# Separate tiles for the samples' keys and values in a two-layer hybrid decoder step

## The chip, the core and the metric

The kernel is written in Bass with the Tile framework and runs on one NeuronCore of one Trainium2 chip. The metric is the device time of one launch in microseconds. One execution was also recorded by the hardware profiler; all rows below come from that recording.

## What is computed

The reference is one inference step of a two-layer trunk for two groups of tokens that share the weights: a prompt of 256 tokens and 8 samples of one token each with a past of 1024 tokens. In each layer:

```python
x += g1 * W_out [ NSA(h) ++ SSD(h) ],  h = RMSNorm(x) * (1 + s1) + b1
x += g2 * ConvFFN(RMSNorm(x) * (1 + s2) + b2)
```

The scales and shifts come from a modulation projection of a conditioning vector (the `ada` weights). NSA is attention with 8 query heads over 2 key/value heads of width 64 in three branches: compressed blocks, selected blocks and a sliding window, mixed by gates. For a sample, the selected branch reads 1024 past positions (8 pages of 128 positions, addressed through a page table, in an order that differs for each sample) with one block of 64 masked off by the selection, and the sliding branch reads a stored state of 512 positions. SSD is a Mamba-2 scan with 8 heads, 2 groups of B and C and a state of 64; for a sample it is one step: the state of 8 x 64 x 64 is decayed, the outer product of x and B is added, and the result is read with C. The outputs are the two groups of tokens and all new states; the sliding state is among them, so every sample's stored keys and values are copied to an output as well as read.

## The kernel before

All arithmetic is at float32 accuracy. The large projections split each operand into a rounded high part and a remainder (`split`, one ScalarE and one VectorE instruction, type float32r) and do three matmuls for each product of 128 x 128 weights with 264 tokens. Smaller products, among them everything in the samples' attention, are plain float32 matmuls, which the profiler shows as two records each.

A layer (`layer`) runs: the norm; a projection for gates; 6 tiles of the convolved x/B/C (a loop over `m`); 10 tiles of keys, values and queries (a second loop over `m`); the attention and state-space stretch; the half of the output projection that depends on the attention; the second norm; and the feed-forward stage with its 44 up-projection and 22 down-projection tiles. In both loops over `m`, `next(side, None)` issues the next pair of modulation weights (two loads of 512 KB and 16 small matmuls), and `next(first, None)` does the next unit of the samples' compressed keys and values (`compress`). In layer 0 these units run inside the loops, on a pool `cmp0` of their own which `done()` closes behind the second loop; then the pool `attn0` opens in its place. In layer 1 the units have run in the feed-forward stage of layer 0, and `attn1` opens at the start of the layer. The modulation weights use two or three buffers, depending on the pool.

The attention and state-space stretch is written as Python generators: `samples` (S), `prompt` (P), `blocks` (B), `gating` (Z), the state space with its gate and output projection (M), and modulation (A). A string of letters, `SEQ`, tells which generator advances next. This is the program order. The framework's scheduler then orders each engine's instructions ahead of the run: among those that its cost model holds ready, the one that is earliest in program order goes first, so that a load can be issued well ahead of its place in the source. On the chip each engine, and each queue that issues transfers (SP for loads, GpSimd for stores), runs that fixed order and waits at an instruction whose inputs or buffer are not there. All scheduling helpers record their instructions from one line, L117, so the rows below are told apart by tile names: `psat`, `psmm`, `pso` and `psfl` are the accumulation banks, `page` the samples' keys and values, `qz` their queries, `mam` the masked B and C, `ada` and `cpg` modulation weights and compressed pages, `st` the weight tiles, `wst` the sliding state, `slcc` the paged cache.

The samples' attention goes through three stages `i`: pages 0 to 3, pages 4 to 7, and the sliding state. Each stage needs a tile of keys and values for each of the 8 samples (`fetch`, 512 KB): four page loads of 128 KB each, every one behind a register load of its page number, or one load of 512 KB from the sliding state, which is at once stored to the output from the same tile. There are 8 such tiles. `scores(i)` does 8 matmuls of a sample's queries (32 columns) with 512 positions, into four groups of 32 output partitions; `values(i)` does 64 small matmuls and, after each half of the samples, fetches the tiles of the next stage into the buffers just read.

## Time and profile before

| | |
|---|---|
| median of 3 runs | 1052.64 us (1051.48 to 1057.06) |
| profiled execution | 1040.78 us, of which the recorded span is 1039.0 us |
| mean granted TensorE clock | 0.945 of full speed |
| TensorE / VectorE / ScalarE / GpSimd busy | 949.7 / 650.7 / 487.4 / 167.8 us |
| HBM read / written | 204.70 / 14.25 MB |

Busy shares are averages over stages with different limits. Granted clock 1.00 is 2.4 GHz, 0.50 is 1.2 GHz. PE is TensorE, PEld its weight loads, DVE VectorE, ACT ScalarE, POOL GpSimd; SPq and POOLq are the queues on which SP and GpSimd issue transfers.

### The profile page before, as it was taken

What the parts mean: (1) busy time and instruction counts of PE and PEld (TensorE: products, weight loads), DVE (VectorE), ACT (ScalarE), POOL (GpSimd) and SP (SyncE); (2) the same over time, 40 slices, a digit from 0 to 9 for tenths busy, and PEclk for the clock granted to TensorE, in tenths of its full rate; (3) what the DMA queues carried; (4) which work ended last, traced back from release to release, by engine and by line L of the source; (5) the groups of instructions that cost most, each with busy time, mean ns of one, the idle gap of its engine ahead of it and who ended that gap; (6) DMA issues with size and microseconds to landing.
All of it is one profiled execution on the core that took longest, in us unless ns stands there. A gap on an engine that the chain in (4) does not pass through costs nothing.

```text
span 1039.0 us, 21345 instructions
## 1 busy us (share of the span) xinstructions
PE 949.7 (91%) x7864; PEld 803.7 (77%) x7864; DVE 650.7 (63%) x1429; ACT 487.4 (47%) x1042; POOL 167.8 (16%) x337
## 2 busy tenths in 40 slices
PE   4599998988997998999999989998999799999996
PEld 2368997653585998999999868875447599999995
DVE  1386643867677665676754575485665687777553
ACT  1356543533444555555634344454244366666441
POOL 2000100225221101001101112031421221111110
PEclk9699999999997999999999989997599899999998
DMA  9987488246757786756675578725283835666651
GB/s 357 313 278 266 158 265 292 94 129 225 270 171 254 232 301 216 238 194 220 210 251 174 183 279 301 244 83 158 91 354 96 330 124 182 183 183 183 194 163 42
DMA packets 101258, 220.35 MB, mean 212 GB/s; under 512 B 11682, under 2 KB 54562, under 8 KB 101026
## 3 DMA queue, kind: packets, MB, share of 16 engines
q1 hardware_dynamic: 97058, 205.28, 59.8%
q0 software_dynamic: 3520, 13.17, 3.1%
q8 instruction: 62, 1.02, 0.4%
q10 hardware_dynamic: 576, 0.54, 0.2%
q14 instruction: 42, 0.34, 0.1%
HBM read 204.70 MB, written 14.25 MB: 211 GB/s over the span
## 4 chain that ended last, share of the span: by engine, by line
PE 76%; DMA 11%; DVE 7%; ACT 3%; issue 2%; SPq 1%; POOL 0%; DVEq 0%; ACTq 0%; POOLq 0%
PE psmm L117 40%; PE psat L117 22%; PE pso L117 10%; PE psfl L117 4%; DMA st<-in_cw_dram 3%; DMA ada<-in_ada_dram 3%; DVE wlo L117 2%; DMA cpg<-in_ada_dram 2%; DMA st<-in_wup_dram 1%; DMA page<-in_wst_dram 1%; DVE s L117 1%; SPq L117 1%; ACT whi L117 1%; DVE rs L117 1%; ACT psc L117 1%
## 5 line engine op out<-in xcount | busy, mean ns | idle before, releaser
L117 DVE TENSOR_TENSOR wlo<-st,whi 128x1024 fp32r<-128x1024 f32 (+1 forms) x204 | 232.7, 1142 | 152.6 <-ACT whi L117 149.1
L117 ACT ACTIVATE whi<-st 128x1024 fp32r<-128x1024 f32 (+1 forms) x204 | 201.6, 990 | 217.5 <-PE psmm L117 150.2
L117 PE MATMUL psmm<-hhi,whi 128*128 128x264 f32 x800 | 233.7, 293 | 3.3 <-ACT whi L117 1.4
L117 PE MATMUL psmm<-hhi,wlo 128*128 128x264 f32 x800 | 228.5, 286 | 1.1 <-DVE wlo L117 1.1
L117 PE MATMUL psmm<-hlo,whi 128*128 128x264 f32 x800 | 228.2, 286 | 0.0
L117 PEld LDWEIGHTS psmm<-hhi,whi 128*128 128x128 f32 x800 | 151.4, 189 | 17.0 <-ACT whi L117 5.2
L117 PEld LDWEIGHTS psmm<-hhi,wlo 128*128 128x128 f32 x800 | 150.9, 189 | 5.2 <-DVE wlo L117 2.4
L117 PEld LDWEIGHTS psmm<-hlo,whi 128*128 128x128 f32 x800 | 151.5, 190 | 2.4 <-issue 2.0
L117 PE MATMUL psmm<-act,whi 128*128 128x264 f32 x704 | 128.5, 284 | 0.0
L117 PEld LDWEIGHTS psmm<-act,whi 128*128 128x128 f32 x704 | 108.9, 188 | 1.6 <-issue 1.6
L117 PE MATMUL psat<-hhi,whi 128*128 128x264 f32 x352 | 100.8, 286 | 2.2 <-ACT whi L117 2.2
L117 PE MATMUL psat<-hhi,wlo 128*128 128x264 f32 x352 | 100.5, 286 | 1.0 <-DVE wlo L117 1.0
L117 PE MATMUL psat<-hlo,whi 128*128 128x264 f32 x352 | 100.6, 286 | 0.0
L117 PE MATMUL psmm<-act,wlo 128*128 128x264 f32 x352 | 99.9, 284 | 0.0
L117 PE MATMUL pso<-whi,cwh 128*128 128x252 f32 x256 | 74.8, 292 | 8.7 <-ACT whi L117 8.0
L117 PE MATMUL pso<-wlo,cwh 128*128 128x252 f32 x256 | 74.1, 290 | 1.8 <-DVE wlo L117 1.8
L117 PE MATMUL pso<-whi,cwl 128*128 128x252 f32 x256 | 73.6, 287 | 0.0
L117 PEld LDWEIGHTS psat<-hhi,whi 128*128 128x128 f32 x352 | 67.1, 191 | 2.5 <-ACT whi L117 2.5
L117 POOL COPY fout<-xr 128x26 f32<-128x26 f32 x44 | 28.1, 639 | 247.0 <-ACT xr L117 247.0
L117 PEld LDWEIGHTS psat<-hhi,wlo 128*128 128x128 f32 x352 | 66.7, 190 | 1.2 <-DVE wlo L117 1.2
L117 PEld LDWEIGHTS psat<-hlo,whi 128*128 128x128 f32 x352 | 67.2, 191 | 0.0
L117 PEld LDWEIGHTS psmm<-act,wlo 128*128 128x128 f32 x352 | 66.1, 188 | 0.0
(305 smaller groups left out, 1579.5 us busy)
## 6 DMA issues: line engine op xcount, KB each, us to landing
st<-in_wup_dram SPq DMA_DIRECT2D x88, 512.0 KB, 3.9
ada<-in_ada_dram SPq DMA_DIRECT2D x80, 512.0 KB, 5.2
st<-in_wdn_dram SPq DMA_DIRECT2D x44, 512.0 KB, 3.6
st<-in_win_dram SPq DMA_DIRECT2D x40, 512.0 KB, 4.9
page<-in_slcc_dram SPq DMA_DIRECT2D x128, 128.0 KB, 2.7
cpg<-in_ada_dram SPq DMA_DIRECT2D x16, 512.0 KB, 9.4
st<-in_cw_dram SPq DMA_DIRECT2D x16, 512.0 KB, 5.9
cpg<-in_cmpc_dram SPq DMA_DIRECT2D x64, 128.0 KB, 3.7
```

The costliest lines, as they stand in the source:

```text
L117: ins = f(*a, **k)
```

## The change

Keys and values get tiles of their own: 8 of 256 KB for keys (`pk`) and 8 for values (`pv`), the same memory in all. `fetch(b)` loads one of them: four page loads of 64 KB, or half of the sliding state. The keys of the next stage are fetched as soon as a stage's scores have been computed, the values after `values` as before. The first 16 fetches (`prefetch`) are spread over both loops over `m`, and in layer 0 the compressed units are finished and `attn0` is opened at the second step of the second loop. The 8 score matmuls of a stage are issued as one unbroken run (`together`: the first is ordered as before, the others directly behind it, in reverse sample order, so that the run begins when the last tile is there). The stores of the sliding state are no longer issued with the load but after `values(2)`, in program order, 16 of 256 KB. The B and C rows of the samples are split into a high part and a remainder, 16 rows in place of 8, and broadcast by a one-pass float32r matmul in place of a float32 one. `SEQ` is as it was.

```diff
--- before.py
+++ after.py
@@ -92,6 +92,7 @@
     ov_n, ov_j = np.arange(NCMP), np.arange(16)
     add("overlap", (16 * ov_n[:, None] < 64 * ov_j[None] + 64) & (16 * ov_n[:, None] + 32 > 64 * ov_j[None]))
     add("sum4", np.tile(np.eye(32), (4, 1)))
+    add("eye8", np.tile(np.eye(8), (2, 1)))
     add("iota", np.broadcast_to(np.arange(16.0), (128, 16)))
     return np.concatenate(parts, 1)
 
@@ -498,23 +499,25 @@
 
 
         order = (0, 2, 4, 6, 1, 3, 5, 7)
-        ring = []
-
-        def fetch():
-            n = len(ring)
+        ring, kept = ([], []), []
+
+        def fetch(b):
+            n = len(ring[b])
             i, s = n // NS, order[n % NS]
             if i > 2:
                 return
-            t = ph([1024], "page", PAGES)
+            t = ph([512], ("pk", "pv")[b], NS)
             if i == 2:
-                load(t, I["wst"][l, s])
-                store(O["wst"][l, s], t)
-                v = t.rearrange("p (a c f) -> p a c f", a=2, c=4)
-                ring.append((v[:, 0], v[:, 1]))
+                load(t, I["wst"][l, s, :, 512 * b:512 * b + 512])
+                kept.append((O["wst"][l, s, :, 512 * b:512 * b + 512], t))
             else:
-                v = t.rearrange("p (c a f) -> p c a f", a=2, c=4)
-                load_pages(v, I["slcc"][l], s, 0, 2, 4 * i, 4)
-                ring.append((v[:, :, 0, :], v[:, :, 1, :]))
+                load_pages(t.rearrange("p (c a f) -> p c a f", a=1, c=4), I["slcc"][l], s, b, 1, 4 * i, 4)
+            ring[b].append(t.rearrange("p (c f) -> p c f", c=4))
+
+        def prefetch():
+
+            if len(ring[1]) < NS:
+                fetch(len(ring[0]) // NS)
 
 
         first = iter(()) if early is None else early()
@@ -568,6 +571,8 @@
                 next(side, None)
             for _ in range(EARLY):
                 next(first, None)
+            if pb is not None:
+                prefetch()
             o = mtile(I["win"][l, 10 + m], h)
             r = sb([291], "xr", 2)
             G.memset(r[:, 0:3], 0.0)
@@ -607,8 +612,12 @@
                 next(side, None)
             for _ in range(EARLY):
                 next(first, None)
-            if pb is not None and len(ring) < PAGES:
-                fetch()
+            if m == 5 and pb is None:
+                run(first)
+                done()
+                pb = begin("attn0")
+            if pb is not None:
+                prefetch()
             o = mtile(I["win"][l, m], h)
             if m < 4:
                 S.activation(q[:, m, :], o[:, :T], AF.Copy, scale=0.125)
@@ -626,11 +635,7 @@
             PE.transpose(o[:8, 256:384], kv[:, m, TP:], ident)
             S.activation(vt[:, b], o[:, :256].rearrange("p (t f) -> p t f", t=2), AF.Copy)
             S.activation(vn[:8, b], o[:8, 256:384], AF.Copy)
-        run(first)
         run(side)
-        if pb is None:
-            done()
-            pb = begin(f"attn{l}")
 
         def samples():
 
@@ -657,8 +662,8 @@
                           stop=s % 2 == 1)
             slf = small([2], 1, "slf")
             V.tensor_copy(slf, selfp[:, :2])
-            while len(ring) < PAGES:
-                fetch()
+            while len(ring[1]) < NS:
+                prefetch()
             pc = small([NCMP], 1, "pc")
             V.tensor_tensor(pc, sp_[:, :NCMP], K["cbias"], op=OP.add)
             st4 = small([8], 1, "st4")
@@ -708,9 +713,10 @@
 
             def scores(i, sc):
                 o = sx()
-                for n, s in enumerate(order):
-                    c = s // 2
-                    PE.matmul(o[32 * c:32 * c + 32, :], qz[:, s, :], ring[NS * i + n][0], start=s % 2 == 0, stop=s % 2 == 1)
+                together([(o[32 * (s // 2):32 * (s // 2) + 32, :], qz[:, s, :], ring[0][NS * i + n], s % 2 == 1, s % 2 == 0)
+                          for n, s in reversed(list(enumerate(order)))])
+                for _ in range(NS):
+                    fetch(0)
                 V.tensor_tensor(sc, sc, o, op=OP.add)
 
             def transposed(sc, pT):
@@ -731,10 +737,10 @@
                     for ch in range(4):
                         for c in range(4):
                             rows = slice(32 * c, 32 * c + 32)
-                            PE.matmul(Ov[rows, sp, :], pT[:, ch, rows], ring[NS * i + 4 * sp + c][1][:, ch, :],
+                            PE.matmul(Ov[rows, sp, :], pT[:, ch, rows], ring[1][NS * i + 4 * sp + c][:, ch, :],
                                       start=sp == 0 and ch == 0 and not cmp, stop=sp == 1 and ch == 3, skip_group_check=True)
                     for c in range(4):
-                        fetch()
+                        fetch(1)
                 if out is None:
                     out = small([128], 1, "ov" + "s-w"[i])
                     V.tensor_scalar(out, Ov[:, 0, :], K["rmask"][:, 0:1], None, op0=OP.mult)
@@ -802,6 +808,8 @@
             for _ in range(WAITS[4]):
                 yield
             ov = values(2, pT, None, True)
+            for dst, t in kept:
+                tc.keep_in_program_order(store(dst, t))
             yield
             vrp = sx()
             PE.matmul(vrp[:, :256], K["sels"][:8, :], vn[:8].rearrange("p b f -> p (b f)"), start=True, stop=True)
@@ -1097,16 +1105,21 @@
             S.activation(dec_s, ov_[:, :, 1, :], AF.Copy)
             V.tensor_tensor(dtx, dtx, xc[:, 0:4, 259::4], op=OP.mult)
             o = mb()
+
+            xs = ph([2, 16], "xs", 1, F32R)
+            split(xc[:, 4:6, 259::4], xs[:, :, :8], xs[:, :, 8:])
             for i in range(2):
-                PE.transpose(o[:8, i * 128:(i + 1) * 128], xc[:, 4 + i, 259::4], ident)
+                PE.transpose(o[:16, i * 128:(i + 1) * 128], xs[:, i, :].bitcast(F32), ident)
             bc = small([2, 128], 1, "bc")
-            S.activation(bc[:8], o[:8, :256].rearrange("p (b n) -> p b n", b=2), AF.Copy)
+            S.activation(bc[:16], o[:16, :256].rearrange("p (b n) -> p b n", b=2), AF.Copy)
+            oner = ph([128], "oner", 1, F32R)
+            S.activation(oner[:16], ones[:16], AF.Copy)
             ys = small([4, NS], 1, "ys")
-            bds = [ph([1024], "mam", 2) for _ in range(2)]
+            bds = [ph([1024], "mam", 2, F32R) for _ in range(2)]
             for g in range(2):
-                V.tensor_tensor(bds[g][:8].rearrange("p (b s n) -> p b s n", b=2, s=NS),
-                                bc[:8, :, 64 * g:64 * g + 64].unsqueeze(2).to_broadcast([8, 2, NS, 64]),
-                                ident[:8, :8].unsqueeze(1).unsqueeze(3).to_broadcast([8, 2, NS, 64]), op=OP.mult)
+                V.tensor_tensor(bds[g][:16].rearrange("p (b s n) -> p b s n", b=2, s=NS),
+                                bc[:16, :, 64 * g:64 * g + 64].unsqueeze(2).to_broadcast([16, 2, NS, 64]),
+                                K["eye8"][:16].unsqueeze(1).unsqueeze(3).to_broadcast([16, 2, NS, 64]), op=OP.mult)
             for g in range(2):
                 yield
                 h0 = slot("st", [2, NS, 64])
@@ -1115,7 +1128,7 @@
                 u = slot("st", [2, NS, 64])
                 for b in range(2):
                     o = mb()
-                    PE.matmul(o, ones[:8, :], bds[g][:8, 512 * b:512 * b + 512], start=True, stop=True)
+                    PE.matmul(o, oner[:16, :], bds[g][:16, 512 * b:512 * b + 512], start=True, stop=True)
                     yield
                     ov_ = o.rearrange("p (s n) -> p s n", s=NS)
                     for i in range(2):
@@ -1295,7 +1308,7 @@
     _o += int(np.prod(_s))
 
 WB = (3, 3, 4)
-PAGES, PSC = 8, 3
+PSC = 3
 BANKS = (4, 2)
 LAG = 2
 WAITS = (0, 0, 0, 1, 1)
```

`together` was there already, for the modulation weights:

```python
    def together(calls):
        for n, (out, w, a, start, stop) in enumerate(calls):
            if n == 0:
                PE.matmul(out, w, a, start=start, stop=stop)
                continue
            with tc.high_priority():
                tc.keep_in_program_order(PE.matmul(out, w, a, start=start, stop=stop))
```

## Rows read from the trace of the kernel before

**Rows 1.** The page's busy time of each engine, share of the span, instructions.
```profile
PE 949.7 (91%) x7864; PEld 803.7 (77%) x7864; DVE 650.7 (63%) x1429; ACT 487.4 (47%) x1042; POOL 167.8 (16%) x337
```

**Rows 2.** Attention stretches: length; busy PE, PEld, DVE, ACT, POOL; clock; DMA share; GB/s.
```profile
165.00:304.00 139.00, 124.27 (x1049) 80.36 (x1048) 93.16 (x260) 57.58 (x172) 35.57 (x60) 0.95 0.56 189
670.00:808.00 138.00, 126.31 (x975) 81.76 (x975) 88.87 (x256) 55.94 (x168) 34.11 (x60) 0.86 0.44 154
```

**Rows 3.** The chain that ended last: start, length, what (four pieces).
```profile
314.73 6.01 DMA st<-in_wup_dram
...
546.37 46.73 PE psmm L117 x384
...
629.57 7.15 DMA ada<-in_ada_dram
...
752.46 10.99 DMA page<-in_wst_dram
```

**Rows 4.** Score stages, `page` alone: length; busy PE, PEld, POOL; clock, DMA share, GB/s.
```profile
195.00:199.00 4.00, 2.96 (x16) 0.53 (x16) 0.00 (x0) 1.00 0.11 43
232.00:244.50 12.50, 6.12 (x16) 0.75 (x16) 0.00 (x0) 0.86 0.74 222
255.00:274.50 19.50, 8.05 (x16) 1.10 (x16) 4.34 (x8) 1.00 1.02 394
690.00:696.00 6.00, 3.17 (x16) 0.45 (x16) 0.00 (x0) 1.00 0.27 89
732.00:736.00 4.00, 3.64 (x16) 0.60 (x16) 0.00 (x0) 0.50 0.02 4
754.00:773.00 19.00, 8.34 (x16) 1.10 (x16) 4.30 (x8) 1.00 1.03 409
```

**Rows 5.** TensorE in order of time: start, length, what, count.
```profile
269.83 1.04 PE L117 MATMUL psat<-page,qz 128*32 128x512 f32 x2
...
692.07 1.06 PE L117 MATMUL psat<-page,qz 128*32 128x512 f32 x8
```

**Rows 6.** B and C, `mam` alone: length; busy PE, PEld, DVE, ACT; clock and DMA.
```profile
230.00:242.00 12.00, 5.40 (x8) 1.37 (x8) 1.58 (x2) 0.00 (x0) 0.77 0.77 234
730.00:744.00 14.00, 7.89 (x8) 2.16 (x8) 1.31 (x2) 0.00 (x0) 0.50 0.09 37
```

**Rows 7.** Busy time by stretch, columns as in rows 2.
```profile
258.00:272.00 14.00, 13.49 (x69) 6.46 (x66) 7.33 (x27) 4.12 (x14) 4.67 (x11) 1.00 1.02 386
...
310.00:330.00 20.00, 13.00 (x64) 10.35 (x64) 14.64 (x41) 7.88 (x17) 4.01 (x3) 0.66 0.76 272
...
780.00:800.00 20.00, 17.94 (x185) 14.06 (x181) 10.80 (x39) 9.28 (x25) 3.72 (x8) 0.91 0.20 66
```

**Rows 8.** Transfers by issue: count, size, median us to landing.
```profile
page<-in_slcc_dram SPq DMA_DIRECT2D x128, 128.0 KB, 2.7
...
cpg<-in_cmpc_dram SPq DMA_DIRECT2D x128, 64.0 KB, 2.7
```

**Rows 9.** SP's issue queue in order of time: start, length, what.
```profile
154.99 13.21 SPq L117 DMA_DIRECT2D page<-in_slcc_dram  x20
...
169.23 0.88 SPq L117 DMA_DIRECT2D ada<-in_ada_dram  x2
...
216.29 20.33 SPq L117 DMA_DIRECT2D page<-in_slcc_dram  x32
...
352.83 8.31 SPq L117 DMA_DIRECT2D cpg<-in_cmpc_dram  x15
...
624.41 1.93 SPq L117 DMA_DIRECT2D page<-in_slcc_dram  x4
...
629.14 0.81 SPq L117 DMA_DIRECT2D ada<-in_ada_dram  x2
```

**Rows 10.** GpSimd in order of time; in brackets the wait before.
```profile
770.16 0.53 POOL L511 DMA_DIRECT2D out_wst_dram<-page  x1 [1.96 <-DMA page<-in_wst_dram]
770.73 1.45 POOL L117 TENSOR_SCALAR psc<-psc,psm 128x256 f32<-128x256 f32 x3
```

## The prediction

> **What bounds the kernel now.** The page's engine line comes first: TensorE is busy 949.7 of the 1039.0 us, VectorE 650.7, ScalarE 487.4 [rows 1]. So TensorE sets the pace, and a change pays where it takes work or waits off that engine. All four edits lie in the attention stretches, so the second view is the busy time by stretch: 165 to 304 us in layer 0 and 670 to 808 us in layer 1 [rows 2]. There TensorE is busy 124.27 of 139 and 126.31 of 138 us. It idles 14.7 and 11.7 us, so the stretches are 89 to 92% TensorE. Layer 1 runs them at a mean granted clock of 0.86, which mixes the two levels, 2.4 and 1.2 GHz.
>
> The third view is the chain that ended last. It has a DMA piece of 10.99 us at 752.46 for the sliding-window tiles [rows 3]. That looks like 11 us to win, but in the 19 us around it the score matmuls of that tile alone kept TensorE busy for 8.34 us [rows 4]: the chain names what released a late instruction, and TensorE did other work meanwhile. So I don't count the piece as a saving. What counts is what TensorE itself no longer does.
>
> **Scores in runs.** A score stage is 8 matmuls (16 records), and there are three stages in each layer. Their busy times, six windows, are 2.96, 6.12 and 8.05 us in layer 0 and 3.17, 3.64 and 8.34 us in layer 1, together 32.28 us [rows 4]. Same 16 records each time, so the spread is order and clock. A run of 8 records takes 1.06 us, and a pair alone 1.04 us [rows 5]: four samples write four different groups of 32 output partitions and run side by side, but only when nothing stands between them. An unbroken stage is then two such runs, 2.0 us at the full clock, or 3.64 us at the half clock (the 732 to 736 window, already unbroken, clock 0.50). For after I take 2.0 us for the first and third stages and 2.8 us, the middle of the two clocks, for the second: 4 x 2.0 + 2 x 2.8 = 13.6 us. Saved: 18.7 us (17.0 to 20.3 with the second stages at the slow or the fast end). Of this the third stages give 8.05 + 8.34 - 4.0 = 12.4 us, the others 6.3 us.
>
> **One-pass B and C.** Eight matmuls of 512 columns in full float32 (16 records) take 5.40 and 7.89 us, together 13.28 us [rows 6]. In the replaced type the trace has 384 matmuls of 264 columns in 46.73 us, 0.122 us each [rows 3]; 512 columns scale to 0.236 us, 1.9 us for the eight. That is the lower end, for a dense stream at full clock. These eight stand alone among waits, so the upper end is half of a lone float32 pair, 1.04 / 2 = 0.52 us, with the half clock in one layer 0.52 x 4 + 1.04 x 4 = 6.2 us. I take 3.5 us, nearer the stream. Saved 9.8 us (7.1 to 11.4). Added in each layer, ahead of these matmuls: a split (one ScalarE and one VectorE instruction) and a ScalarE copy of the ones. By the mean instruction of the layer 1 stretch, 55.94 / 168 = 0.33 us and 88.87 / 256 = 0.35 us [rows 2], the split puts 0.7 us on the path of each layer, 1.4 us in all; the copy waits for nothing and hides under the same engine's idle time. The masked product reads 16 rows where it read 8 with the same length per row, which I price at nothing (0 to 2 us, by doubling the 2.89 us that VectorE spent in those windows at worst).
>
> **How much of the TensorE cut shows.** The third score stages lie where TensorE is dense: it is busy 13.49 of the 14 us from 258 to 272 [rows 7]. I count all 12.4 us. The other 6.3 + 9.8 = 16.1 us lie where the softmax chains of the prompt and of the samples leave holes, and shorter work uncovers longer holes. I count 0.6 of it, 9.7 us; the bounds are 0.3 and 1.
>
> **Separate tiles, loaded earlier.** A page load now fetches keys or values alone, so there are 128 issues of 64 KB in place of 64 of 128 KB in each layer, 128 more in all. The queue pays per issue, not per byte: 32 page issues of 128 KB take 20.33 us, 0.635 each, and 15 of 64 KB in another stage 8.31 us, 0.554 each; landing takes 2.7 us for either size [rows 8, 9]. So SP carries 128 x 0.635 = 81 us more, 41 in each layer. In the attention stretch of layer 0 this has room. The second stage's 32 pages now go out from 216.29 to 236.62, once the first values have been read [rows 9]. After the change its keys may go out right behind the first scores, which end by 199 [rows 4], and are done by 219; the values follow in the place of today's pages, done by 240 and landed by 243, before even the scores of that stage are over today (244.5). In the first projections of layer 1 it is tight. There the page issues lie between pairs of modulation weights on two buffers, and the chain already waits for such a pair, 7.15 us at 629.57 [rows 3]. Four page issues end at 626.34, and the pair goes out at 629.14 with one weight load between [rows 9]; the gap of some 2.4 us just takes four more issues (4 x 0.554 = 2.2 us). So I take +2 us, between nothing and all of 32 x 0.55 = 17.6 us.
>
> The Trainium skill (DMA: Bandwidth & Descriptors, Rules for kernel authors) speaks against this edit: coalesce small transfers, since small ones pay mostly overhead. The trace agrees that the halves cost as much to issue and to land as the wholes did. By the fixed 2 us that the same page gives for one DMA (Anatomy of one DMA, the GpSimd path), if nothing hid it, the sum would grow by 128 x 2 = 256 us, an estimate from that page. By the issue row SP's time grows by the 81 us above, most of it beside TensorE's work.
>
> **Pool opened earlier in layer 0.** Page loads already run there from 154.99 [rows 9], ahead of the attention stretch and of the place in the source where the pool is opened, since the planner moves them up. Opening it earlier in the source adds little. I take nothing, with the bounds under the queue's rival.
>
> **Stores late.** Now each store of sliding state stands in GpSimd's queue until its load lands, and softmax scaling waits behind it: one store goes out at 770.16 after 1.96 us of waiting, and three scalings follow at 770.73 [rows 10]. That wait goes, which helps the prompt branch; I count it inside the 0.6 above. The 16 stores of 256 KB in each layer then run after the last values, past the third scores' window (274.5 in layer 0 [rows 4]). 4.19 MB at the 386 GB/s of a full DMA stretch (258 to 272, share 1.02) is 10.9 us [rows 7]. Layer 1 has room (share 0.20 from 780 to 800). In layer 0 the DMA share is 0.76 from 310 to 330, and the chain waits 6.01 us for an up-projection tile [rows 3, 7]. I take +1 us, between 0 and 10.9.
>
> **The sum.** -12.4 - 9.7 + 1.4 + 2 + 1 = -17.7 us against this execution's own 1040.78 us (span 1039.0 and 1.8 around it): 1023.1 us, or 1.7% less. The three runs shown have a median of 1052.64 us, 1.1% above the profiled one, so the same share gives 1034.7 us. I forecast 1035.
>
> **The rivals.** Each is priced against the median.
> 1. *Holes swallow the cut.* VectorE is busy 88 to 93 us in each stretch [rows 2], and if the prompt's softmax chain sets the pace, only some 5 us of the cut show: 1048. For it: the half clock in layer 1 comes from such holes. Against: the stretches are 90% TensorE [rows 2]. Chance 0.13.
> 2. *Slower: SP's issue queue takes over.* Place: the first projections of layer 1 (17.6 us), and layer 0 at 169, where 20 page issues end at 168.20 and a modulation pair goes out at 169.23; another 32 issues ahead of it are 20.3 us [rows 9]. All exposed: -17.7 - 2 + 17.6 + 20.3 = +18.2, or 1071. It decides the sign from 20 us exposed. Against: the planner orders by readiness, and the values are needed only behind the first scores, 30 us later [rows 4]. Chance 0.12.
> 3. *Late stores collide.* All 10.9 us exposed in layer 0: -7.8, or 1045. Against: with its keys there early the samples' branch can end sooner, and the stores with it. Chance 0.10.
> 4. *The clock follows.* The whole cut of 28.5 us shows, layer 1's second scores run at 2.4 GHz (0.8 us more), and other work there gains some 8 us: a mean clock of 0.86 over 138 us [rows 2] is 38.6 us at the half clock, of which 8 us is under half of what could come back. With the queue's term at nothing: -28.5 - 0.8 - 8 + 1.4 + 1 = -34.9, or 1017. Chance 0.08.
>
> **Chances and range.** The forecast keeps 0.57. Under 0.5% (5 us) a measurement of this kernel can't tell a change from none. Faster by more than that: 0.54 of the forecast's 0.57, all of rival 4, half of rival 1, 0.07 of rival 3: 0.75. Slower: rival 2 and 0.01 of rival 1: 0.13. The same: 0.12. The range runs from rival 4's side, 1015, to 1052, which leaves out the slow rival and the tail below, under 2 in 10.
>
> **What would show it.** Right: every score stage is one run of 16 records in 2 to 3.7 us; the B and C records are 8, not 16, under 0.6 us each at full clock; no DMA piece for the sliding tiles on the chain; no GpSimd wait on their loads; both stretches shorter by 7 to 12 us; the projections of layer 1 within 3 us of before. Wrong: the stretch from 592 to 670, before the attention of layer 1, grows, with TensorE waiting for modulation weights behind page issues; or the feed-forward stage of layer 0 starts as late after its attention as now plus the stores; or the busy time falls by 28 us and idle time grows by as much.

## The result and the profile after

The change made the kernel slower: 1082.42 us, median of 4 runs (1080.33 to 1091.17), beside 1052.06 us for the kernel before on the same chip, 30 us more. The ratio over the fast runs of each kernel alone, which leaves out runs in a slower state of the chip, is 1.0361 (95% interval 1.0300 to 1.0422), some 38 us of 1052. The forecast was 1035 us, with 0.13 on slower. The profiled execution after took 1080.33 us, span 1078.6; that of before took 1040.78, 1.1% under that kernel's median, so I compare kernels by ratios and use the two traces only to place the loss.

**Where the time went.** The busy time by stretch of the kernel after, columns as in [rows 2]. The stretches are cut at the same work in each trace: from the first score stage of layer 0 to its second norm, its feed-forward stage, from there to the first score stage of layer 1, and on to the second norm of layer 1.

```profile
209.80:343.10 133.30, 108.88 (x844) 73.07 (x843) 84.39 (x227) 51.70 (x142) 37.65 (x57) 0.81 0.54 176
343.10:622.50 279.40, 271.54 (x2296) 255.73 (x2296) 176.97 (x320) 143.24 (x264) 29.78 (x73) 0.98 0.68 223
622.50:732.90 110.40, 94.45 (x801) 78.65 (x801) 58.41 (x144) 43.60 (x102) 10.44 (x32) 0.95 0.66 213
732.90:862.90 130.00, 106.02 (x858) 71.05 (x857) 86.08 (x236) 53.20 (x150) 41.34 (x65) 0.84 0.56 190
```

The same stretches of the kernel before:

```profile
195.50:318.40 122.90, 106.47 (x848) 66.58 (x847) 88.22 (x235) 53.30 (x146) 38.05 (x54) 0.94 0.55 183
318.40:595.90 277.50, 270.68 (x2296) 255.10 (x2296) 176.88 (x320) 143.20 (x263) 29.86 (x73) 0.98 0.68 223
596.00:690.30 94.30, 87.31 (x785) 74.50 (x785) 57.33 (x147) 44.65 (x108) 15.09 (x37) 0.96 0.72 249
690.30:823.40 133.10, 119.45 (x877) 74.74 (x876) 84.19 (x233) 52.15 (x143) 36.14 (x53) 0.85 0.54 191
```

And the difference, with the stretch ahead of them from the timelines:

| stretch | before us | after us | difference |
|---|---|---|---|
| first norm of layer 0 to its first scores | 176.5 | 190.2 | +13.7 |
| first scores to second norm, layer 0 | 122.9 | 133.3 | +10.4 |
| feed-forward, layer 0 | 277.5 | 279.4 | +1.9 |
| first norm of layer 1 to its first scores | 94.4 | 110.4 | +16.0 |
| first scores to second norm, layer 1 | 133.1 | 130.0 | -3.1 |

They add up to 38.9 of the 39.6 us between the spans. Three stretches lose, and they are those in which SP's queue carries pages. The only one that gains is the attention of layer 1: TensorE's busy time falls there from 119.45 to 106.02 us, and 3.1 of those 13.4 us show.

How far one execution can be trusted for this shows when the traces of all kernels below are set side by side. Two of the five stretches separate cleanly. Ahead of the first scores, every kernel that loads its pages whole takes 175.2 to 180.2 us in layer 0 and 93.3 to 97.8 in layer 1, and every kernel with the page issues doubled on SP takes 188.5 to 191.6 and 108.5 to 116.5 (the one that issues half of them from GpSimd belongs to neither). The attention stretches don't separate: 122.9 to 144.0 against 133.3 to 138.7 us in layer 0, and 121.0 to 142.7 against 130.0 to 144.6 in layer 1. The 122.9 us of the kernel before are the shortest of all, and kernels level with it by the ratio take up to 133.9 there. So +13.7 and +16.0 are losses that the change makes; the +10.4 can be the luck of one execution, and so can the -3.1.

**The queue.** SP's issue queue after, layer 0, against [rows 9]:

```profile
133.79 17.67 SPq L118 DMA_DIRECT2D pk<-in_slcc_dram  x28
151.56 0.61 SPq L118 DMA_DIRECT2D st<-in_win_dram  x1
...
165.50 20.64 SPq L118 DMA_DIRECT2D pv<-in_slcc_dram  x28
186.24 0.85 SPq L118 DMA_DIRECT2D st<-in_win_dram  x2
187.18 0.86 SPq L118 DMA_DIRECT2D ada<-in_ada_dram  x2
...
210.82 19.65 SPq L118 DMA_DIRECT2D pk<-in_slcc_dram  x32
230.58 0.37 SPq L118 DMA_DIRECT2D st<-in_ssm_dram  x1
231.55 21.71 SPq L118 DMA_DIRECT2D pv<-in_slcc_dram  x32
253.37 3.69 SPq L118 DMA_DIRECT2D pk<-in_wst_dram  x8
257.11 0.44 SPq L118 DMA_DIRECT2D st<-in_ssm_dram  x1
```

Read it by what stands behind each block of pages. 28 key pages hold a projection weight (`st`) for 17.67 us, 28 value pages hold two weights and a modulation pair for 20.64. In the second stage the second half of the samples' state (`st<-in_ssm`) goes out at 257.11; before it went out at 236.67, straight behind the 32 pages. Of these 20.4 us, 14.3 are the late start of the whole stretch; counted from the first scores it goes out after 47.4 us in place of 41.2. Half the bytes cost the same issue: 0.61 to 0.74 us against 0.635 [rows 9], though they land in 2.0 and 1.9 us in place of 2.7 [rows 8].

What waits for these loads, by the waits of TensorE from 130 to 350 us (total, times, longest), and then TensorE and GpSimd in order of time:

```profile
PE psmm L118 <- ACT whi L118: 12.3, 4, 4.7
PE psat L118 <- ACT s L118: 5.8, 1, 5.8
```
```profile
158.00 0.59 PE L118 MATMUL psmm<-hhi,whi 128*128 128x264 f32 x1 [4.71 <-ACT whi L118]
...
191.94 0.59 PE L118 MATMUL psmm<-hhi,whi 128*128 128x264 f32 x1 [4.63 <-ACT whi L118]
...
277.87 3.68 PE L118 MATMUL psat<-s,cst 128*2 128x264 f32 x8 [5.78 <-ACT s L118]
```
```profile
267.91 1.62 POOL L118 TENSOR_SCALAR psc<-psc,psm 128x128 f32<-128x128 f32 x4 [7.89 <-DVE psm L118]
269.50 1.90 POOL L118 TENSOR_TENSOR st<-st,decs 128x1024 f32<-128x1024 f32 x1
```

The releaser named for the first is ScalarE, but ScalarE only splits a weight (`whi`) that SP issued late: the weights that went out at 151.56 and 186.24, behind the two blocks of 28 pages, are those for which TensorE waits 4.71 and 4.63 us. Some 10.4 of the 12.3 us lie ahead of the first scores, in the stretch that lost 13.7.

The other wait is for the gate (`s`), which needs the samples' state. Its eight matmuls start 68.1 us after the first scores, where before they started after 61.3. GpSimd updates the state at 269.50 (before at 243.18), but not as soon as the load is there: it comes to the update straight from a softmax scaling at 267.91, which had waited 7.89 us for VectorE. So the trace shows a late place in GpSimd's order, and that the late load is the reason for that place is not shown. The matmuls then take 3.68 us where before they were through in 2.0, and the clock is lower: the mean granted clock of the layer 0 stretch is 0.81, and of its counterpart before 0.94. So TensorE's busy time did not fall there (108.88 after, 106.47 before).

In layer 1 the projections run in step with the pages. SP's queue there, after:

```profile
668.65 1.18 SPq L118 DMA_DIRECT2D ada<-in_ada_dram  x2
670.38 1.93 SPq L118 DMA_DIRECT2D pv<-in_slcc_dram  x4
672.40 0.38 SPq L118 DMA_DIRECT2D st<-in_win_dram  x1
673.36 2.27 SPq L118 DMA_DIRECT2D pv<-in_slcc_dram  x4
675.73 0.37 SPq L118 DMA_DIRECT2D st<-in_win_dram  x1
```

One projection weight goes out every 3 us behind four value pages, where before the last four weights went out together in 4.54 us, from 651.26 on. TensorE waits 6.7 us for splits of such weights in this stretch; before it waited 0.3.

**What the change did achieve.** The first three score stages of TensorE in order of time, against [rows 4, 5], and a B and C record, against [rows 6]:

```profile
209.75 1.92 PE L118 MATMUL psat<-pk,qz 128*32 128x512 f32 x16
246.07 0.76 PE L118 MATMUL psat<-mam,oner 16*128 16x512 f32 x1 [0.38 <-DVE mam L118]
246.76 3.64 PE L118 MATMUL psat<-pk,qz 128*32 128x512 f32 x16
...
268.78 3.31 PE L118 MATMUL psat<-pk,qz 128*32 128x512 f32 x16
```

Every stage is one run of 16 records; the six take 17.9 us in place of 32.28. The four B and C records of a layer take 2.28 us of TensorE in place of 5.40 and 7.89. No tile of the sliding state is waited for. So these records take 23.1 us less, of the 28.5 that the prediction counted. TensorE's busy time over the whole execution did not fall with them: it is 953.1 us for 949.7 [rows 1], at a mean granted clock of 0.923 for 0.945.

### The profile page after: what moved, and what is told of

Its sections match the earlier page's. It is cut to its first block, busy times and chain, and to the rows that moved or that the text cites. A ratio compares the mean times of both kernels' runs of the same rounds, so it can differ in the third digit from the quotient of the medians.

```text
span 1078.6 us, 21791 instructions
## 1 busy us (share of the span) xinstructions
PE 953.1 (88%) x7856; PEld 815.7 (76%) x7856; DVE 654.4 (61%) x1431; ACT 488.3 (45%) x1046; POOL 173.9 (16%) x353
## 4 chain that ended last, share of the span: by engine, by line
PE 63%; DVE 7%; DMA 6%; ACT 3%; issue 2%; SPq 1%; POOL 0%; DVEq 0%; ACTq 0%; POOLq 0%
PE psmm L118 35%; PE psat L118 20%; PE pso L118 5%; PE psfl L118 3%; DMA ada<-in_ada_dram 2%; DVE wlo L118 2%; DMA st<-in_wout_dram 2%; ACT whi L118 1%; DMA st<-in_cw_dram 1%; DVE rs L118 1%; DVE st L118 1%; DMA st<-in_wup_dram 1%; ACT psc L118 1%; DVE x L118 1%; SPq L118 1%
## 5 line engine op out<-in xcount | busy, mean ns | idle before, releaser
L118 PE MATMUL psmm<-hhi,whi 128*128 128x264 f32 x800 | 236.1, 296 | 22.9 <-ACT whi L118 21.5
L118 PE MATMUL psmm<-hhi,wlo 128*128 128x264 f32 x800 | 232.0, 290 | 7.7 <-DVE wlo L118 7.7
L118 PEld LDWEIGHTS psmm<-hhi,wlo 128*128 128x128 f32 x800 | 152.7, 191 | 13.6 <-DVE wlo L118 10.4
L118 DVE SCALAR_TENSOR_TENSOR xa<-xr,halfw,xa 128x280 f32<-128x280 f32 (+1 forms) x124 | 63.1, 509 | 9.5 <-ACT xa L118 7.4
```

What stands on the lines that cost most here:

```text
L118: ins = f(*a, **k)
```

## The experiments

Each is one edit to the kernel before or to the changed one. Ratios are to the kernel before, run on the same chip in the same session (medians 1044 to 1051 us).

**The issues alone.** The kernel before, each page issued as two halves into the same tile.

```diff
-                load_pages(v, I["slcc"][l], s, 0, 2, 4 * i, 4)
+                for b in range(2):
+                    load_pages(v[:, :, b:b + 1], I["slcc"][l], s, b, 1, 4 * i, 4)
```


> The kernel before, with each page load issued as two loads of 64 KB (keys, then values) into the same tile: 128 issues more, nothing else changed in the source. Theory 1 (SP's issue queue: page issues stand ahead of projection weights, modulation weights and the samples' state): 15 to 35 us slower than before, with TensorE waiting for weight tiles ahead of the first scores. Theory 2 (the pinned score runs and the order that the planner makes around them): within 5 us of before, since nothing of that is in this kernel. Theory 3 (rows of 512 B move slower than rows of 1 KB): slower too, but with a DMA share near 1 where TensorE waits, not with the queue busy.

Measured 1107.91 us, 1.0607 (1.0528 to 1.0686): the issues alone lose more than the whole change does, and more than the 15 to 35 us that I expected. Its queue in layer 0, TensorE there, and the busy time around TensorE's wait (columns as in [rows 2]):

```profile
155.28 34.10 SPq L117 DMA_DIRECT2D page<-in_slcc_dram  x52
189.48 0.85 SPq L117 DMA_DIRECT2D st<-in_win_dram  x2
```
```profile
194.41 0.59 PE L117 MATMUL psmm<-hhi,whi 128*128 128x264 f32 x1 [13.65 <-ACT whi L117]
```
```profile
176.00:191.00 15.00, 4.57 (x31) 3.53 (x30) 10.29 (x31) 5.42 (x20) 5.53 (x11) 0.79 0.43 109
```

0.656 us each, and TensorE waits 13.65 us for the weight behind them. The mean DMA share is 0.43 meanwhile, so it is not the transfers that are full, which theory 3 asked for. Nothing was moved here and no buffer split, so doubling the issues is enough for the loss. It also doubles the pieces, the unbroken stretches of memory that a load is made of (128 in an issue, whole or half). The first of the four tries below doubles the pieces of the pages and not their issues, and the stretches ahead of the first scores take 180.2 and 97.8 us there; here they take 190.3 and 113.5.

**Is it the register load?** As the last, but each four page numbers are read into registers once and serve both halves (`load_halves`).

```diff
+        for a in range(2):
+            for i, v in enumerate(ids):
+                load(dst[:, i, a:a + 1], src[bass.ds(v, 1), :, a:a + 1, :].rearrange("o p a f -> (o p) a f"))
```


> The kernel before with each page loaded as two 64 KB halves into the same tile, as in the run with the issues doubled, but each group of four page numbers is read into registers once and serves both halves. If the price of an issue is the DMA instruction itself, the loss stays near that run's 59 us: 1095 to 1110. If it is mostly the register load ahead of it, under half of it stays: 1060 to 1078, and a page issue in the queue takes some 0.3 to 0.4 us in place of 0.64.

1099.44 us, 1.0508 (1.0425 to 1.0592). Half the register loads are gone and the price of an issue is not: 0.639 us.

```profile
155.06 33.22 SPq L117 DMA_DIRECT2D page<-in_slcc_dram  x52
```

**The parts of the change, divided.** First everything but the loads (runs, one-pass B and C, late stores; whole pages as before), then the loads alone (separate tiles, the early pool and `prefetch`; scores, B and C and stores as before).

```diff
-                for n, s in enumerate(order):
-                    c = s // 2
-                    PE.matmul(o[32 * c:32 * c + 32, :], qz[:, s, :], ring[NS * i + n][0], start=s % 2 == 0, stop=s % 2 == 1)
+                together([(o[32 * (s // 2):32 * (s // 2) + 32, :], qz[:, s, :], ring[NS * i + n][0], s % 2 == 1, s % 2 == 0)
+                          for n, s in reversed(list(enumerate(order)))])
```


> The kernel before with scores in runs, one-pass B and C and late stores, and the loads as before: theories 1 and 3 expect 1034 to 1044 us, 8 to 18 us faster than before, which is the gain that the forecast gave to these parts. Theory 2 expects it 5 to 15 us slower than before.

> The changed kernel's loads alone (separate tiles, early pool, prefetch in both loops), with scores, B and C and stores as before. Theory 1: the whole loss and none of the gain, 1085 to 1105 us. Theory 2: 1045 to 1060 us. Theory 3 as theory 1.

Without the loads 1055.34 us, 1.0072 (1.0039 to 1.0106); the loads alone 1091.68 us, 1.0413 (1.0335 to 1.0491), some 43 us. So the loads carry the loss, and the other edits are worth nothing without them either: the first of the two is some 8 us slower, within the 5 to 15 of theory 2. Its trace shows one reason; the late stores, which are tried alone below, are in it too. Its waits of TensorE in the two attention stretches, and TensorE in order of time:

```profile
PE psat L118 <- DMA page<-in_wst_dram: 11.0, 1, 11.0
```
```profile
PE psat L118 <- DMA page<-in_wst_dram: 10.5, 1, 10.5
```
```profile
267.05 3.64 PE L118 MATMUL psat<-page,qz 128*32 128x512 f32 x16 [11.02 <-DMA page<-in_wst_dram]
```

The run of the third stage stands in TensorE's order where the first single matmul stood, needs the last tile, and everything behind it waits. Single matmuls took the tiles as they landed, between other work.

**Another queue.** The changed kernel, the values' pages issued from GpSimd.

```diff
-                load_pages(t.rearrange("p (c a f) -> p c a f", a=1, c=4), I["slcc"][l], s, b, 1, 4 * i, 4)
+                load_pages(t.rearrange("p (c a f) -> p c a f", a=1, c=4), I["slcc"][l], s, b, 1, 4 * i, 4,
+                           *((ET.SP, load), (ET.Pool, nc.gpsimd.dma_start))[b])
```


> The changed kernel with the page loads of the values issued from GpSimd's queue, page numbers read there too: same transfers, same rows, 128 issues fewer on SP. Theory 1: 15 to 30 us faster than the changed kernel, 1052 to 1067 us, if GpSimd's own work isn't held up. Theories 2 and 3: within 5 us of the changed kernel (1082 us).

1068.55 us, 1.0201 (1.0120 to 1.0281), about 17 us better than the changed kernel by the ratios. In its profiled execution the stretch ahead of the first scores of layer 0 takes 175.2 us (before 176.5, after 190.2), and the gate starts 61.9 us behind the first scores (61.3 and 68.1): the loss of 13.7 us goes whole, with as many issues, bytes and tiles as in the changed kernel. That is the strongest sign that its place is SP's queue. The attention of layer 0 is no shorter for it, 135.9 us. Layer 1's input still takes 107.3 us in place of 94.4, though SP issues 32 page loads there as before; the first projection weight behind them goes out 30 us after the norm (at 645.10), where before it went out after 13 (at 609.07). So in layer 1 the number of SP's issues is not the whole cause; the place of the key pages among the weights is a rival that no run settles. The Trainium skill (Perfetto Trace Analysis, DMA Optimizations) says that balancing transfers across the engines that issue them may help when generating descriptors is the bottleneck; here it gave back under half of the loss.

**Where the values' pages stand.** The changed kernel with the pool opened where it was before, and the values' first loads behind the projections.

```diff
-            if pb is not None:
-                prefetch()
+            if pb is not None and len(ring[0]) < NS:
+                fetch(0)
...
+            while len(ring[0]) < NS:
+                fetch(0)
             while len(ring[1]) < NS:
-                prefetch()
+                fetch(1)
```


> The changed kernel with the first stage's values loaded behind the projections and the pool opened where it was before; tiles, runs, B and C and late stores as in the changed kernel. Theory A (the 33 and 16 us that the projections of both layers lost come from value loads placed ahead of weight tiles): 10 to 25 us under the changed kernel, 1058 to 1073 against a before of about 1048, with the first score stage of layer 1 less than 35 us behind that of before. Rival (the loss is the number of issues, wherever they stand): 1073 to 1085.

1078.53 us, 1.0242 (1.0185 to 1.0300): the interval only touches that of the changed kernel. In its trace layer 0 starts its first scores as late (210.2), and so does layer 1 (731.6, 41 us behind before, where theory A wanted less than 35). The 32 issues have moved behind the projection's first tiles and hold the next ones:

```profile
690.70 19.84 SPq L118 DMA_DIRECT2D pv<-in_slcc_dram  x32
710.63 1.32 SPq L118 DMA_DIRECT2D st<-in_win_dram  x3
```

So the values' place in the source isn't the cause, as the rival has it; whether it is worth some 10 us of the total stays open.

**The third run without its wait.** The kernel before with all three runs and one-pass B and C; the third stage reads a resident tile. This leaves the sliding keys' part of the scores out: it prices a third stage that waits for no load, and is no replacement for the step.

```diff
-                    PE.matmul(o[32 * c:32 * c + 32, :], qz[:, s, :], ring[NS * i + n][0], start=s % 2 == 0, stop=s % 2 == 1)
+                together([(o[32 * (s // 2):32 * (s // 2) + 32, :], qz[:, s, :], cst[:, :512].rearrange("p (c f) -> p c f", c=4) if i == 2 else ring[NS * i + n][0], s % 2 == 1, s % 2 == 0)
+                          for n, s in reversed(list(enumerate(order)))])
```


> The kernel before with runs in all three score stages and one-pass B and C, stores and loads as before; the third stage's scores read a resident constant tile in place of the sliding keys, so that they wait for no load (this leaves the sliding keys' part of the scores out). Theory A (a third run is worth its 12 us of TensorE time if its keys cost nothing to have early): 1028 to 1040 against a before of about 1047. Rival (TensorE's cut falls into holes here too): 1043 to 1050.

1036.20 us, 0.9876 (0.9823 to 0.9929). 13 us, and it is the only kernel here whose interval lies below 1. Its third run:

```profile
251.07 2.67 PE L118 MATMUL psat<-cst,qz 128*32 128x512 f32 x16
...
754.44 1.89 PE L118 MATMUL psat<-cst,qz 128*32 128x512 f32 x16
```

It ends 20 and 16 us before the third scores of before do (274.0 and 772.1, in the windows of [rows 4]). Set beside before's single profile the gain is in layer 1 alone, whose attention takes 121.0 us in place of 133.1, while that of layer 0 takes 127.0 in place of 122.9. The better partner is the second kernel of the next experiment, which differs in the third stage alone: there the two stretches take 133.9 and 125.3, and both are longer.

**The cheap cuts.** The kernel before with one-pass B and C alone (the diff above, from `xs` to `oner`), with runs in the first two stages as well, and with late stores besides.

```diff
+                if i < 2:
+                    together(mms)
+                else:
+                    for out, w, a, start, stop in reversed(mms):
+                        PE.matmul(out, w, a, start=stop, stop=start)
```


> The kernel before with one-pass B and C alone. If its cut lies on the path as the prediction counts it (9.8 us at 0.6, less 1.4 for the split): 1043 to 1047 against a before of about 1050. If holes swallow it: 1048 to 1052. If the split and the copies ahead of it delay the samples' branch: over 1052.

> The kernel before with runs in the first and second score stages and one-pass B and C; third stage, loads and stores as before. If late stores took back what these two save: 4 to 10 us faster than before. If holes swallow these cuts: within 3 us of before.

> The kernel before with one-pass B and C, late stores, and runs in the first and second score stages only; the third stage keeps eight single score matmuls, and the loads are as before. Theory A (in the run with all but the loads, the third run stood on TensorE and waited 11.0 and 10.5 us for the last sliding-state tile, and that wait ate the cut): without that run the wait is gone, and 6 to 15 us of the cut show: 1034 to 1044 against a before of about 1050. Theory B (what remains of the cut falls into holes of the softmax chains, or the one-pass split costs what it saves): 1047 to 1056.

0.9999 (0.9958 to 1.0041), 1.0018 (0.9990 to 1.0047) and 1.0046 (1.0007 to 1.0086). By the prediction's count some 16 us of TensorE work go, and no time. By the trace of the second kernel, the records of its first two stages and of B and C take 13.5 us less, but TensorE's busy time over the whole execution is 945.5 us for 949.7, at a granted clock of 0.932 for 0.945. My theory for the second kernel, that the third run's wait had eaten a cut that else shows, fell: without that run nothing shows either.

**Late stores alone.**

```diff
-                store(O["wst"][l, s], t)
+                kept.append((O["wst"][l, s], t))
...
             ov = values(2, pT, None, True)
+            for dst, t in kept:
+                tc.keep_in_program_order(store(dst, t))
```


> The kernel before with the sliding-state stores issued after the last values, and nothing else. Theory A (the stores' 4.2 MB run beside the loads of the output projection's weights; in the run with the first two runs TensorE waits 3.1 and 2.7 us there for a split weight, and the chain 7.07 us for its load): slower by 5 to 11 us. Rival (the wait on GpSimd's queue that goes away pays for it): within 4 us of before or faster.

1059.14 us, 1.0107 (1.0058 to 1.0156), 11 us. Its waits of TensorE behind the last values of layer 0, and its chain there:

```profile
PE psmm L117 <- ACT whi L117: 5.3, 1, 5.3
```
```profile
294.85 9.48 DMA st<-in_wout_dram
```

Before, that piece of the chain is 4.21 us and TensorE waits for no split weight there. The stores leave at 289 us, just as the weights of the output projection are wanted. In the changed kernel this price is not to be seen:

> The changed kernel with the sliding state stored behind its load again. Late stores alone cost 11 us in the kernel before. If the parts add up: 8 to 12 us under the changed kernel, 1067 to 1075 against a before of about 1048. If the queue's delays hide the stores' price here: within 4 us of the changed kernel, 1078 to 1087.

1089.88 us, 1.0362 (1.0309 to 1.0416), the ratio of the changed kernel itself. Its median is 3 us above the rival's band. And in the company of runs and one-pass B and C late stores cost some 3 us (1.0046 against 1.0018, with intervals that overlap). The parts don't add up; that the stores fall beside something else that is late would explain it, and is not shown.

**Can early sliding keys be had without the pages' issues?** Four tries. First: eight lasting tiles, pages whole, keys and values in separate halves of a tile, so that a sliding key half waits only for the second scores; runs, one-pass B and C, late stores.

```diff
+            if i == 2:
+                load(t[:, 512:], I["wst"][l, s, :, 512:])
+            else:
+                load_pages(t.rearrange("p (a c f) -> p c a f", a=2, c=4), I["slcc"][l], s, 0, 2, 4 * i, 4)
...
+                if i == 1:
+                    for n, s in enumerate(order):
+                        load(tiles[n][:, :512], I["wst"][l, s, :, :512])
```


> Runs in all three score stages, one-pass B and C, late stores, and pages loaded whole as before (one issue of 128 KB each); only the sliding state is loaded in two halves, its keys as soon as the second scores have read the tile, its values after the second values: 16 issues more in all where the changed kernel has 144. Theory A (page issues doubled on SP's queue are the loss; the third run needs only early sliding keys): the third run no longer waits, both layers' projections start as before, and the cut shows: 1025 to 1040. Rival (the cut is lost whatever the loads do): 1047 to 1056. If the early sliding keys hold SP's queue ahead of weight tiles: over 1056, with the projections or the gate late as in the changed kernel.

1069.64 us, 1.0248 (1.0168 to 1.0329). The third run found its keys, and lost them again to the second stage, whose pages are now written in two pieces for each partition, 256 for an issue in place of 128:

```profile
216.07 28.10 SPq L118 DMA_DIRECT2D page<-in_slcc_dram  x32
```

0.878 us each in place of 0.635 [rows 9]; TensorE waits 9.1 us for these pages. Late stores are in this kernel as well. Second: pages laid out as before, sliding halves written between their pieces, stores at the load. Third: the same, with the returned state copied from memory to memory behind the first scores. And that copy alone in the kernel before.

```diff
+            load(tiles[n % NS].rearrange("p (c a f) -> p c a f", a=2, c=4)[:, :, b, :],
+                 I["wst"][l, s, :, 512 * b:512 * b + 512].rearrange("p (c f) -> p c f", c=4))
...
+                        tc.keep_in_program_order(store(O["wst"][l, s], I["wst"][l, s]))
```


> Runs in all three stages and one-pass B and C; pages loaded whole in the layout of before; only the sliding state in two halves, its keys as soon as the second scores have read the tile, written between the pages' pieces (512 pieces of 512 bytes for each half); stores behind each half's load. In the run with sliding keys the second stage's page issues took 0.88 us each in place of 0.635, with 256 pieces each in place of 128. Theory A (that was its loss, with the late stores): here the second stage's pages go out in some 20 us again, the sliding issues take about 1.2 us each, an estimate from those two rows, in a stretch where the queue is free, and the third run finds its keys: 1030 to 1045 against a before of about 1047. Rival (the sliding issues hold the output projection's weights, or the cut doesn't show): 1047 to 1065.

> The kernel of the run with interleaved sliding halves, but the returned sliding state is copied from memory to memory right after the first scores, where the transfers are slack (DMA share 0.31 from 200 to 230 us before), so that no store waits on GpSimd's queue for a load. Theory A (that run lost its 13 us to the stores and to the state loads held behind the sliding issues; TensorE waited 8.9 us for the gate's state in layer 1): 1032 to 1044 against a before of about 1048. Rival (the sixteen sliding issues themselves hold the state load and the output projection's weights): 1046 to 1056.

> The kernel before with the returned sliding state copied from memory to memory right after the first scores, and nothing else. If stores at the load cost nothing where they are: within 4 us of before. If their waits on GpSimd's queue cost something: 3 to 10 us faster. If the copies collide with the second stage's page loads: slower.

1.0035 (0.9994 to 1.0077), 1.0082 (1.0042 to 1.0123) and 0.9982 (0.9942 to 1.0023). So the stores' waits cost nothing in the kernel before, and taking them out of the second try does not bring its gain. In both the third run ends as early as with free keys, at 253.3 and 756.9 us in the second try and at 254.8 and 762.7 in the third, and no gain shows: an early end of this stage is not enough by itself. The second try's queue and TensorE in layer 1:

```profile
741.37 5.36 SPq L118 DMA_DIRECT2D page<-in_wst_dram  x8
746.78 1.66 SPq L118 DMA_DIRECT2D st<-in_ssm_dram  x1
...
753.59 10.38 SPq L118 DMA_DIRECT2D page<-in_wst_dram  x8
```
```profile
770.25 3.28 PE L118 MATMUL psat<-s,cst 128*2 128x264 f32 x8 [8.94 <-ACT s L118]
```

Early keys again stand ahead of the samples' state, and the gate is late, as in the changed kernel. But GpSimd's state update waits only 0.18 us for that load here; it then stands behind a store that waits 4.97 us for a sliding tile. In the third try, without such stores, TensorE still waits 7.2 us for the gate in layer 1. What holds the gate in both tries stays open.

**The third run at another place.** The kernel before with the third run alone, two steps later in the program, and in two runs of four tiles each.

```diff
-WAITS = (0, 0, 0, 1, 1)
+WAITS = (0, 0, 2, 1, 1)
```
```diff
+                for k in (0, 4):
+                    together(mms[k:k + 4][::-1])
```


> The kernel before with a run in the third score stage alone, written two steps later, so that TensorE's order has the gate's matmuls ahead of it; loads, stores, B and C and the other scores as before. Theory A (the third run lost 11.0 and 10.5 us to waiting because it stood ahead of work that was ready; later it finds its tiles): the wait is under 4 us in each layer, the stage takes 2 to 3.7 us, and 3 to 12 us show: 1036 to 1046 against a before of about 1049. Rival (the softmax behind the scores then starts later than with single matmuls, and the end of the branch with it): 1047 to 1056.

> The kernel before with the third score stage in two runs of four matmuls, each of four samples on four groups of output partitions, at the place of the first single matmuls; nothing else changed. Theory A (a run needs only its own tiles, and the halving of the time comes from four side by side): each half takes 1.0 to 1.8 us, the waits for sliding tiles are less than the 11 us of the whole run, and the time is within 5 us of before on either side. Rival (in TensorE's order the halves still stand ahead of ready work): slower by 5 to 12 us.

1.0010 (0.9973 to 1.0048) and 1.0185 (1.0130 to 1.0240). The later run has its tiles and hardly waits, first the trace of the later run, then that of the halves:

```profile
273.15 1.92 PE L117 MATMUL psat<-page,qz 128*32 128x512 f32 x16
...
769.00 3.64 PE L117 MATMUL psat<-page,qz 128*32 128x512 f32 x16 [1.07 <-DMA page<-in_wst_dram]
```
```profile
270.32 1.40 PE L117 MATMUL psat<-page,qz 128*32 128x512 f32 x8 [2.79 <-DMA page<-in_wst_dram]
...
780.95 1.94 PE L117 MATMUL psat<-page,qz 128*32 128x512 f32 x8 [5.02 <-DMA page<-in_wst_dram]
```

The later run ends at 275.1 and 772.6 us, no sooner than the single matmuls did. Its records take 5.6 us for the 16.4 of [rows 4], the stage's end stays, and nothing shows. With free keys it ended some 20 us sooner, and 13 us showed. The halves wait 4.0 and 6.8 us for their tiles, less than the whole run's 11.0 and 10.5, but the loss of 1.8% is beyond what either theory allowed, and these waits don't account for it: TensorE is busy 974.1 us in that execution for 949.7 before, at a granted clock of 0.907 for 0.945.

## Why the prediction was wrong

**What bounds the kernel.** The first step already failed: "So TensorE sets the pace, and a change pays where it takes work or waits off that engine" reads a busy share as a limit. One-pass B and C and the first two runs took 13.5 us off TensorE's records, and 0 showed (0.9999, 1.0018) where I counted 9.7. Whether waits elsewhere or the lower clock (0.932 for 0.945) took it, the traces don't tell apart. The Trainium skill (Perfetto Trace Analysis, Identifying the Most-Contended Engine) says that TensorE's busy share is no good measure of how close one is to roofline; that is about headroom, and no run here measures it. Rival 1 had the holes for the whole cut and a chance of 0.13.

**Scores in runs.** The six stages take 17.9 us where I counted 13.6: both third stages ran in 3.31 and 3.43 us and not in 2.0, at a granted clock of 0.58 and 0.56.

**The third stages, 12.4 us counted whole.** The size agrees with the 13 us of free keys, but that is luck, since the reason was not right: the later run takes 10.8 us off TensorE's records with the stage's end where it was, and gives nothing (1.0010). What pays is not fully shown. With free keys the stage ends some 20 us sooner; but it does so in the second and third tries too, without gain. And at its old place with whole tiles the run costs 11.0 and 10.5 us of waiting, so at that place it needs early keys.

**Separate tiles, +2 us of 0 to 17.6.** 47 us lie between the forecast and the result. 17.7 of them are gains that were counted and did not show; the other 30 are in this term and the next. The loads alone cost some 43 us, and the whole change 38: the parts don't add up exactly. The price of an issue was right (0.61 to 0.74 us for 0.635). The step that failed is "By the issue row SP's time grows by the 81 us above, most of it beside TensorE's work". The projections' weights stand behind the pages on SP's queue, and the stretches ahead of the first scores grew by 13.7 us in layer 0 and 16.0 in layer 1. For layer 1 I took +2, argued from one gap of 2.4 us at 626.34; the measured 16.0 is near the upper bound of 17.6. "In the attention stretch of layer 0 this has room" held for the pages themselves: the last of them goes out 43.5 us after the first scores, where I counted some 44.5, and the second scores start 37.0 us after the first in both kernels. I held the pages against their own deadlines and not what stands behind them. That the stretch lost anything by them is not shown.

**Pool opened earlier, nothing.** As far as the edit goes this stands: with the pool opened late again, layer 0 starts its first scores as late (210.2 against 209.75). But I put the price of the issues themselves in that place under the rival only, and it was +13.7 us.

**Rival 2, 1071, chance 0.12,** is what happened. Its two places and their prices were 17.6 and 20.3 us; measured are 16.0 and 13.7. Where it fell short is its sum, which still took the cuts as gained, 17.7 us which did not show. Its argument against, that the planner orders by readiness, cuts the other way: pages whose buffers are free are ready early, and they went out ahead of weights. That this is why the planner put them there is not shown.

**Late stores, +1 us of 0 to 10.9.** In the kernel before they cost 11, the bound; in the changed kernel nothing that can be measured. The stores that they replace cost nothing where they stood (0.9982 without their waits), so "that wait goes" was no gain.

**One-pass B and C** cost 2.28 us of TensorE in each layer, 4.6 in both, within the bounds of 1.9 and 6.2 and above the 3.5 that I took.

**The rule that spoke against.** The Trainium skill (DMA: Bandwidth & Descriptors, Rules for kernel authors) asks to coalesce small transfers, and calls those under 64 KB mostly overhead. The halves here are of 64 KB, and the runs agree that whole is better: 1.0607 for the same bytes in twice the issues. But they landed sooner than the wholes (2.0 us for 2.7); the price lay on SP's queue. I had weighed the rule, priced the queue at 81 us, and then called most of that hidden.

## What to carry to other kernels

Before adding issues to a queue, list what stands behind them on it and who waits for that; a deadline met by the transfers themselves says nothing of it. An engine that is busy 90% of a stretch is not the bound by that: here 10.8 and 13.5 us less of its records bought nothing. An earlier result is not a gain by itself either; ask what else its user waits for. An unbroken run that begins with its last input holds everything behind it until that input is there, so place it where its inputs have landed. And before a loss is put in a place by one trace of each kernel, see how much that place varies between kernels that are equally fast.

## What the runs showed that was not expected

- The price of an issue with a page number in a register follows the pieces, not the bytes, in these rows: 128 KB in 128 pieces 0.635 us, 64 KB in 128 pieces 0.656, 128 KB in 256 pieces 0.878. Sharing the register loads left it at 0.639.
- It is not a fixed price for a piece: the sliding halves of 512 pieces without a register took 5.36 / 8 = 0.67 us each as keys and 10.38 / 8 = 1.30 as values, in one layer (waits inside such a block are not told apart). I had estimated 1.2.
- The price of a whole against a half sliding tile is the same on the queue: 3.69 us for eight of 256 KB, where the kernel before took 3.77 for eight of 512 KB.
